# Pinned experts' weights on ScalarE's DMA queue, a ring with one more place, and the experts' weighting behind the gather

## The chip, the cores and the metric

The kernel runs on one core of a Trainium2 chip. The metric is device time in microseconds (us) of one execution, the median over several runs. The core has a matrix engine (TensorE, "PE" in the rows), three engines for elementwise work (VectorE "DVE", ScalarE "ACT", GpSimd "POOL"), and SyncE ("SP"), which issues transfers. SP and ScalarE each have a queue for plain transfers; GpSimd issues the indirect ones (gathers and scatters of rows). Every engine takes its own instructions in order.

## The reference

Two layers over a latent sequence of 512 tokens and a context of 256 tokens, width 1024, float32. Each layer has an attention and recurrence mixer and then a hierarchical mixture of experts; layer 0's mixture runs on 768 tokens, layer 1's on 512.

```python
xl = xl + ga1 * (concat([y_na, y_rg, y_diff]) @ w_out[l])
hl2 = rmsnorm(xl, g_ffn[l]) * (1 + sc2) + sh2
...
g_prob = softmax(h @ w_g + b_g)                     # 4 groups
g_top, g_idx = top_k(g_prob, 1)
e_logits = (h @ w_e + b_e).reshape(N, 4, 8)[g_idx]  # 8 experts of the group
e_top, e_idx = top_k(softmax(e_logits), 2)
weight = g_top * e_top / sum(e_top)
y[token] += weight * ((silu(x @ w1[e]) * (x @ w3[e])) @ w2[e])   # 32 experts, 1024 -> 512 -> 1024
xl = xl + ga2 * y
```

All 32 experts of a layer have tokens here, so all of w1, w3 and w2 are read: 6 MB an expert, 192 MB a layer.

## The kernel before

For each layer `program` runs a mixer, then the output projection, then the mixture of experts.

**Output projection and routing.** A loop over 128-token tiles t (six in layer 0, four in layer 1) multiplies by w_out, adds to X (`upd`, L1353), squares the row on ScalarE (L1354), takes the root on GpSimd (L1356, L1357), turns the tile for the router on TensorE with ScalarE copying the turned blocks (`turn_x`), takes the logits (L1402), and in `normed` scales (L1363) and adds the shift (L1364, on VectorE for tiles in `HVV`, else on GpSimd). SP writes the normed tile to memory (L1365). `top2` finds group and experts. After the loop come the one-hot sums: ranks of tokens within their expert, `val` and two clears of the gather buffers on GpSimd (L1439, L1441), the rank product and sum (L1442, L1448, L1449), one one-hot per half tile (L1451) times the tokens' numbers on TensorE (L1452), the experts ordered by count, and the index table `idx_t` (L1475) with `slots` (where results are scattered, L1496 to L1500), `idall` and `idn` (L1503 to L1509). `weights()` turns the router's numbers into each token's weight in its expert (L1783 to L1812): exponentials, a division, a split in three bfloat16 parts (L1795, L1797), products with the one-hots on GpSimd (L1798) and on TensorE (L1802, L1805).

**Experts.** Experts are taken in an order of slots by count. The last three slots always hold experts 29 to 31 (NPIN = 3), whatever their counts; these are called *pinned*, since their weights can be loaded before the routing is known; the order `seq` begins with them. All others are loaded by a number that routing yields (`sid`). For each slot GpSimd gathers token rows (L1832), TensorE turns them (`turn`, L1634, copied by VectorE or ScalarE through `copy`), multiplies by w1 and w3 (`first`), ScalarE and VectorE make the hidden rows (`mid` with its copy L1664, `hidden`), TensorE multiplies by w2 (`second`), and `out` scales and scatters (L1523).

**The ring of weights.** An expert's weights come in six pieces of 1 MB ([128, 2048] float32). Pieces take places in turn from three pools: `wt` (six, shared with the mixer and the projection), `wt2` (opened at the tile loop) and `wt3` (four, opened after it). `NWA` places of `NW2` are opened earlier, in the projection (`wta`); `W0` says where the six of `wt` stand in the turn. That gives 16 places in layer 0 and 18 in layer 1. `eparts` issues a piece: the first `SPIN[l]` pieces on the engine it is called with, the rest on SP. `pin_steps` yields the 18 pieces of the pinned experts: `NWA` in the projection, up to `PINT[l]` in the tile loop, then all but `HELD[l]`; the held ones wait for `idn` (L1509). A build-time planner orders each engine's instructions by when it expects them to be ready; `behind(a, b)` puts a after b on the same engine.

```python
held[0] = (Y if wcount[0] > SPIN[l] else eng).dma_start(...)          # eparts, L1030
for _ in range(8 // nt + 1):
    if wcount[0] < PINT[l]:
        next(ping)                                                   # tile loop
for _ in range(6 * NPIN - wcount[0] - HELD[l]):
    next(ping)                                                       # after the loop
```

Of the kernel before, what the change touches and what calls it, by code (L numbers as in the profile page):

```python
# [13 lines left out]
ALU = mybir.AluOpType  # L14
# [9 lines left out]
NE = 32  # L24
# [31 lines left out]
RGS = (2, 2)  # L56
RGR = (1.0, 0.85)
FLG = (1, 1)
WST = (0, 0)
HELD = (4, 3)  # L60
DMO = ("gsXw", "gsXw")
FLL = (3, 1)
LTS = ("aaatmghsscccbbbbcccccMccocHccc", "")
# [5 lines left out]
CUT = 0  # L69
W67 = ((), ())  # L70
RG0 = (5, 2)
HVV = [(1, 3), (1, 3)]
NP6 = 1
WSV = ((0, 2), (0, 2))
W1S = ((1, 1, 2, 3), (1, 1, 2, 3))
# [12 lines left out]
UE = ("SV", "SV")  # L88
OSV = ((0, 1), (0, 1))
OHV = ((0, 1, 2, 3, 4, 5), (0, 1, 2, 3, 4, 5))  # L90
SPIN = (2, 0)
PINT = (6, 8)
FEX = (0, 0)
DOR = ("asctwfv", "asctwfv")
CHD = ("TV", "TV")
# [7 lines left out]
AHEAD = 1  # L103
CXN = ((2, 0, 0), (0, 0, 2))
XNB = (6, 2)
NW2 = (6, 8)
NWA = (0, 2)
NWS = (9, 9)
W0 = (4, 12)
LAM = (1, 1)  # L110
DIAG = (1, 1)
SCT = (1, 1)
# [138 lines left out]
def program(tc, a, out, dbg=None):  # L251
    nc = tc.nc
# [22 lines left out]
    V, S, G, T = [Chained(e_) for e_ in (nc.vector, nc.scalar, nc.gpsimd, nc.tensor)]  # L275
# [69 lines left out]
        return (pool or wt).tile([128, 2048], dt, name="w", bufs=n)  # L345

    def copy(eng, o, i):
        if eng is S:
            S.copy(o, i)
        else:  # L350
            eng.tensor_copy(o, i)  # L351

    def ada_steps(l, groups=(0, 1, 2)):
        for g in groups:
# [47 lines left out]
    def behind(ins, other):  # L402
        tc.add_manual_dep(ins.ins, other.ins.name,
                          mybir.DependencyInfo(mybir.DependencyClass.NoSync, mybir.DependencyReason.DATA), reason="order")
# [6 lines left out]
    mark = {}  # L411
# [18 lines left out]
    ct = lambda c_, x_, y_: x_ if c_ else y_  # L430
# [5 lines left out]
    def bc(ap, n):  # L436
        return ap.unsqueeze(len(ap.shape)).to_broadcast(list(ap.shape) + [n])
# [13 lines left out]
    for l in range(2):  # L451
# [555 lines left out]
        lg = xp_.tile([128, nt, 36], F32, name="lg")  # L1007
# [305 lines left out]
        gm, m1, m2, t1 = [rk.tile([128, nt], F32, name=n_) for n_ in ("gm", "m1", "m2", "t1")]  # L1313
# [31 lines left out]
        op = P.open(f"op{l}", side="right")  # L1345
# [125 lines left out]
        tk = rt.tile([128, 3, 32], F32, name="tk")  # L1471
# [17 lines left out]
        nd, nm, nr = NDL[l], NML[l], NE - NPIN  # L1489
        assert (nr - nm) % 2 == 0  # L1490
        np_ = (nr - nm) // 2
        ncol = nm + np_ + NPIN
        slots = wk_.tile([128, ncol], I32, name="slots") if SCT[l] else None
        if SCT[l]:
            sf = tk[:, 2]
            V.tensor_copy(slots[:, 0:nd], sf[:, 0:nd])  # L1496
            V.tensor_copy(slots[0:64, nd:nm], sf[0:64, nd:nm])
            V.tensor_copy(slots[0:64, nm + np_:ncol], sf[0:64, nr:NE])
            for i in range(2):
                V.tensor_copy(slots[32 * i:32 * i + 32, nm:nm + np_], sf[0:32, nm + i:nr:2])  # L1500
        idall = wk_.tile([128, ncol], F32, name="idall")
        idn = wk_.tile([128, ncol, nt], F32, name="idn")
        V.tensor_copy(idall[:, 0:nd], idx_t[:, 0:nd])  # L1503
# [106 lines left out]
        class Expert:  # L1610
# [16 lines left out]
            def turn(self):  # L1627
                n = self.cap
                self.xT = wk_.tile([128, 8, 128], F32, name="xT", bufs=2)
                m = min(8, 512 // n)  # L1630
                for q in range(8 // m):
                    pt = mm()
                    for k in range(m):
                        T.transpose(pt[:, n * k:n * k + n], self.xgt[0:n, 128 * (m * q + k):128 * (m * q + k) + 128], ident[0:n, 0:n])  # L1634
                    copy(ct(q, S, V), self.xT[:, m * q:m * q + m, 0:n], pt[:, 0:n * m].rearrange("p (k t) -> p k t", t=n))
                self.p = pss()

            def first(self):
# [139 lines left out]
        wsl = rk.tile([128, nv, 32], F32, name="wsl")  # L1778
        def weights():

            gs = rt.tile([128, nt], F32, name="gs")
            gx = rt.tile([128, nt, 4], F32, name="gx")
            V.tensor_tensor(gx, lg[:, :, 0:4], bc(gm, 4), op=ALU.subtract)  # L1783
            S.activation(gx, gx, AF.Exp)
            V.tensor_reduce(gs, gx, axis=AX.X, op=ALU.add)
            V.tensor_sub(m2, m2, m1)
            S.activation(m2, m2, AF.Exp)
            V.scalar_tensor_tensor(t1, m2, 1.0, gs, op0=ALU.add, op1=ALU.mult)
            wgt = rt.tile([128, 2, nt], F32, name="wgt")
# [189 lines left out]
        for n_ in range(NE + 1):  # L1979
# [18 lines left out]
            if n_ == NE - 1:  # L1998
                mark.clear()
                if not last:  # L2000
                    for c0 in (768, 1024):
                        cut, i_ = chunk(1, c0)
# [125 lines left out]
        for k_ in SEQ[l]:  # L2128
# [4 lines left out]
            else:  # L2133
                combine(*k_)
                if k_[1]:
                    n_, t = k_[0], order[k_[0]]
# [32 lines left out]
```

## Time and profile before

| | us |
|---|---|
| median of three runs | 2021.67 |
| lowest, highest | 2017.29, 2025.94 |
| the profiled execution | 2016.25 |
| its span, first to last instruction | 2014.7 |
| TensorE busy in it | 1688.6 |
| VectorE, ScalarE, GpSimd busy | 902.0, 575.4, 405.3 |
| moved by DMA | 579.20 MB |

All times below are of the profiled execution, in us from the start of its span. Layer 0's experts run from about 520 to 1075, layer 1's from about 1486 to 1985. A busy share is an average over stages with different limits, so the stages are read by themselves. "A <- B" in a view of waits means that A sat idle until B was done; an instruction in a timeline has its start, its length, its engine and line, output <- inputs, and in brackets the idle time before it with what ended it.

### The profile page before, as it was taken

The page shows a single profiled execution, that of the slowest core. Times are in us where ns is not written, and L with a number is a line of the kernel's source. Part 1 is how long each engine was busy: PE and PEld are TensorE (multiplying, and loading weights), DVE is VectorE, ACT ScalarE, POOL GpSimd, SP SyncE. Part 2 cuts the span into 40 slices and gives each one's busy share as a digit, 9 for nine tenths or more (in the row PEclk, how much of TensorE's full clock was granted, in tenths as well). Part 3 has the DMA queues.
Part 4 walks back from the last instruction along what each step waited for, and adds up shares of the span by engine and source line. Part 5 has one row for each costly group of instructions (what it writes and reads, how often), then busy time and mean ns, then how long its engine had stood idle before and what let it go on. Part 6 is the DMA issues. An engine that isn't in the chain of part 4 may idle for free. (4 is left out here: it accounts for less than half of the span.)

```text
span 2014.7 us, 24883 instructions
## 1 busy us (share of the span) xinstructions
PE 1688.6 (84%) x9306; PEld 977.0 (48%) x9306; DVE 902.0 (45%) x1507; ACT 575.4 (29%) x1034; POOL 405.3 (20%) x395
## 2 busy tenths in 40 slices
PE   5998998898688879898985998988969988979763
PEld 3767776676333333333334866766733333323321
DVE  3877544776422222212138588648642122121225
ACT  3563454552101111111124465546311000000111
POOL 1344002443211001000003135114311110110001
PEclk8999999898798999999896999989969999999896
DMA  8537726426899989999895446454579999999994
GB/s 303 198 138 274 271 74 168 118 75 230 336 406 348 413 334 373 414 356 412 337 399 198 141 179 215 149 179 142 209 264 402 405 407 416 411 413 415 417 389 172
DMA packets 153710, 579.20 MB, mean 287 GB/s; under 512 B 18735, under 2 KB 54959, under 8 KB 114673
## 3 DMA queue, kind: packets, MB, share of 16 engines
q1 hardware_dynamic: 142240, 553.35, 72.4%
q0 software_dynamic: 9328, 20.87, 2.9%
q10 hardware_dynamic: 2016, 3.34, 0.5%
q8 instruction: 75, 1.23, 0.2%
q14 instruction: 51, 0.41, 0.1%
HBM read 544.74 MB, written 42.05 MB: 291 GB/s over the span
## 5 line engine op out<-in xcount | busy, mean ns | idle before, releaser
L497 PE MATMUL mm<-hh,w 128*128 128x256 f32 (+1 forms) x960 | 192.5, 345 | 9.2 <-ACT w L433 4.7
L1649 PE MATMUL pss<-w,xT 128*64 128x512 f32 x368 | 173.4, 619 | 7.0 <-DMA w<-in_w_dram 7.0
L1648 PE MATMUL pss<-w,xT 128*64 128x512 f32 x368 | 177.7, 626 | 0.0
L497 PEld LDWEIGHTS mm<-hh,w 128*128 128x128 f32 x960 | 151.0, 194 | 38.6 <-issue 6.4
L1644 PE MATMUL pss<-w,xT 128*32 128x512 f32 x880 | 136.8, 669 | 37.9 <-DMA w<-in_w_dram 37.7
L1832 POOL DMA_INDIRECT xg<-h2d,idx_t x64 | 61.3, 959 | 512.1 <-PE mm L1634 473.6
L1654 PE MATMUL pss<-w,xT 128*128 128x512 f32 x352 | 156.0, 598 | 0.0
L1664 ACT COPY hs<-pss 128x512 f32<-128x512 f32 x53 | 30.9, 582 | 375.7 <-PE pss L1644 224.1
L1523 POOL DMA_INDIRECT yd<-yl,slots x47 | 44.3, 942 | 382.5 <-DVE yl L1568 202.2
L1706 PE MATMUL pss<-w,hT 128*64 128x512 f32 x184 | 102.2, 699 | 9.1 <-DVE hT L1684 8.9
L1654 PEld LDWEIGHTS pss<-w,xT 128*128 128x128 f32 x352 | 65.3, 190 | 89.1 <-issue 83.5
L1684 DVE TENSOR_TENSOR hT<-hT,mm 128x128 f32<-128x128 f32 (+1 forms) x53 | 18.3, 345 | 193.8 <-ACT hT L1683 193.6
L1707 PE MATMUL pss<-w,hT 128*64 128x512 f32 x184 | 101.8, 696 | 0.0
L1564 DVE SCALAR_TENSOR_TENSOR yl<-g,wsl,yl 64x1024 f32<-64x1024 f32 (+2 forms) x32 | 40.8, 1277 | 128.7 <-ACT yl L1559 128.4
L1644 PEld LDWEIGHTS pss<-w,xT 128*32 128x32 f32 x880 | 31.5, 119 | 135.9 <-issue 72.5
L1559 ACT ACTIVATE yl<-g,wsl 64x1024 f32<-64x1024 f32 (+2 forms) x32 | 36.6, 1147 | 209.4 <-DMA yd<-yl,slots 177.3
L497 PE MATMUL mm<-hl,w 128*128 128x256 f32 (+1 forms) x480 | 92.8, 335 | 0.4 <-POOL hl L616 0.4
L1712 PE MATMUL pss<-w,hT 128*128 128x512 f32 x176 | 89.5, 655 | 3.1 <-issue 3.1
L1568 DVE TENSOR_TENSOR yl<-pss,yl 64x512 f32<-64x512 f32 (+1 forms) x44 | 29.6, 687 | 135.5 <-PE pss L1707 74.3
L351 DVE COPY xT<-mm 128x512 f32<-128x512 f32 (+1 forms) x64 | 36.2, 565 | 103.8 <-PE mm L1634 103.1
L497 PEld LDWEIGHTS mm<-hl,w 128*128 128x128 f32 x480 | 75.3, 190 | 10.4 <-POOL hl L616 0.6
L1649 PEld LDWEIGHTS pss<-w,xT 128*64 128x64 f32 x368 | 49.5, 142 | 62.6 <-issue 49.9
(380 smaller groups left out, 3256.2 us busy)
## 6 DMA issues: line engine op xcount, KB each, us to landing
w<-in_w_dram SPq DMA_DIRECT2D x382, 1024.0 KB
w<-in_w_ada_dram SPq DMA_DIRECT2D x48, 1024.0 KB
w<-in_w_in_dram SPq DMA_DIRECT2D x20, 1024.0 KB
yd<-bm SPq DMA_DIRECT2D x20, 512.0 KB
w<-yd SPq DMA_DIRECT2D x10, 1024.0 KB
ks<-st SPq DMA_DIRECT2D x16, 384.0 KB
w<-in_w_out_dram SPq DMA_DIRECT2D x5, 1024.0 KB
h2d<-hp SPq DMA_DIRECT2D x10, 512.0 KB
```

The costliest lines, as they stand in the source:

```text
L497: i_ = T.matmul(o, x_(k), y_(k), start=(n == 0), stop=(n == 23))
L1523: G.indirect_dma_start(out=yd[l][0:2 * nrow, :], out_offset=bass.IndirectOffsetOnAxis(ap=idxt, axis=0), in_=rows, in_offset=None, bounds_c ...
L1559: S.activation(self.u[r], g2[r, 1], AF.Copy, scale=b_)
L1564: (V if eng[1] == "V" else G).scalar_tensor_tensor(self.u[r], g2[r, 0], a_, self.u[r], op0=ALU.mult, op1=ALU.add)
L1644: T.matmul(ph[32 * g:32 * g + 32, 0:512], xT[:, k + g // 2, 0:32], w(k + g // 2), start=(k == 0), stop=(k == 6))
L1648: T.matmul(ph[0:64, 0:512], xT[:, k, 0:64], w1(k), start=(k == 0), stop=(k == 7))
L1649: T.matmul(ph[64:128, 0:512], xT[:, k, 0:64], w3(k), start=(k == 0), stop=(k == 7))
L1654: T.matmul(ph[:, o:o + 512], xT[:, k, :], w(k), start=(k == 0), stop=(k == 7))
L1706: T.matmul(py[0:64, :], hT[:, k, 0:64], w2(k, 0), start=(k == 0), stop=(k == 3))
L1707: T.matmul(py[64:128, :], hT[:, k, 0:64], w2(k, 1), start=(k == 0), stop=(k == 3))
L1712: T.matmul(self.p[:, 512 * hf:512 * hf + 512], hT[:, k, :], w2(k, hf), start=(k == 0), stop=(k == 3))
L1832: G.indirect_dma_start(out=o[0:n_, :], out_offset=None, in_=h2d[l][0:nrow, :], in_offset=bass.IndirectOffsetOnAxis(ap=idxt, axis=0), bound ...
```

## The change

Pins: `SPIN` 18 sends all 18 pinned pieces of a layer through ScalarE's queue, `PINT` 14 asks for up to 14 of them by the end of the tile loop, and `HELD` leaves one (layer 0) or none (layer 1) for after `idn`. Ring: one more early place in each layer (`NW2`, `NWA`), 17 and 19 places, with the `wt` places at other turns (`W0`); the memory comes from a smaller scratch for the descriptors of GpSimd's transfers. Routing: the casts of `slots` and the steps of `weights()` on VectorE go behind the first copy of the first expert's turned rows (`mark["V", "xT"]`), and the eight steps of that expert's `first` stand ahead of `weights()` in the program (`WST` 8). The shift add L1364 goes to VectorE for tiles 4 and 5 in layer 0 and tile 2 in layer 1 (`HVV`).

```diff
-WST = (0, 0)
-HELD = (4, 3)
+WST = (8, 8)
+HELD = (1, 0)
-HVV = [(1, 3), (1, 3)]
+HVV = [(1, 3, 4, 5), (1, 2, 3)]
-SPIN = (2, 0)
-PINT = (6, 8)
+SPIN = (18, 18)
+PINT = (14, 14)
-NW2 = (6, 8)
-NWA = (0, 2)
+NW2 = (7, 9)
+NWA = (1, 3)
-W0 = (4, 12)
+W0 = (7, 9)
...
     def copy(eng, o, i):
-        if eng is S:
-            S.copy(o, i)
-        else:
-            eng.tensor_copy(o, i)
+        return S.copy(o, i) if eng is S else eng.tensor_copy(o, i)
...
         slots = wk_.tile([128, ncol], I32, name="slots") if SCT[l] else None
-        if SCT[l]:
-            sf = tk[:, 2]
-            V.tensor_copy(slots[:, 0:nd], sf[:, 0:nd])
-            V.tensor_copy(slots[0:64, nd:nm], sf[0:64, nd:nm])
-            V.tensor_copy(slots[0:64, nm + np_:ncol], sf[0:64, nr:NE])
-            for i in range(2):
-                V.tensor_copy(slots[32 * i:32 * i + 32, nm:nm + np_], sf[0:32, nm + i:nr:2])
...
-                    copy(ct(q, S, V), self.xT[:, m * q:m * q + m, 0:n], pt[:, 0:n * m].rearrange("p (k t) -> p k t", t=n))
+                    i_ = copy(ct(q, S, V), self.xT[:, m * q:m * q + m, 0:n], pt[:, 0:n * m].rearrange("p (k t) -> p k t", t=n))
+                    if q == 0:
+                        mark["V", "xT"] = i_
...
         def weights():
 
+            m_ = mark["V", "xT"]
+            if SCT[l]:
+                sf = tk[:, 2]
+                behind(V.tensor_copy(slots[:, 0:nd], sf[:, 0:nd]), m_)
+                V.tensor_copy(slots[0:64, nd:nm], sf[0:64, nd:nm])
+                V.tensor_copy(slots[0:64, nm + np_:ncol], sf[0:64, nr:NE])
+                for i in range(2):
+                    V.tensor_copy(slots[32 * i:32 * i + 32, nm:nm + np_], sf[0:32, nm + i:nr:2])
             gs = rt.tile([128, nt], F32, name="gs")
             gx = rt.tile([128, nt, 4], F32, name="gx")
-            V.tensor_tensor(gx, lg[:, :, 0:4], bc(gm, 4), op=ALU.subtract)
+            behind(V.tensor_tensor(gx, lg[:, :, 0:4], bc(gm, 4), op=ALU.subtract), m_)
             S.activation(gx, gx, AF.Exp)
             V.tensor_reduce(gs, gx, axis=AX.X, op=ALU.add)
-            V.tensor_sub(m2, m2, m1)
+            behind(V.tensor_sub(m2, m2, m1), m_)
...
-    nc = bacc.Bacc("TRN2", target_bir_lowering=False, num_devices=1)
+    nc = bacc.Bacc("TRN2", target_bir_lowering=False, num_devices=1, dynamic_dma_scratch_size=4096)
```

## Rows read from the trace of the kernel before

**Rows 1.** TensorE's waits, 520 to 1075: us in total, times, longest.

```profile
PE mm L1678 <- ACT hs L1664: 43.5, 12, 7.3
```

**Rows 2.** TensorE's waits, 1486 to 1985.

```profile
PE pss L1644 <- DMA w<-in_w_dram: 37.7, 16, 4.4
```

**Rows 3.** Waits of SP's queue, 1486 to 1985.

```profile
SPq L1030 <- DMA w<-in_w_dram: 308.1, 151, 6.8
```

**Rows 4.** Windows: engines' busy us (instructions), granted clock, DMA share, GB/s.

```profile
1485.00:1490.00 5.00, 1.89 (x16) 1.80 (x16) 2.11 (x11) 0.00 (x0) 2.60 (x3) 0.50 0.51 152
...
1500.00:1505.00 5.00, 5.00 (x26) 1.76 (x24) 0.62 (x2) 2.25 (x3) 0.87 (x1) 1.00 0.70 231
...
1600.00:1700.00 100.00, 83.98 (x461) 35.64 (x463) 23.49 (x39) 8.78 (x18) 10.47 (x11) 0.94 1.02 411
```

**Rows 5.** VectorE in order of time, layer 0, 440 to 545.

```profile
474.44 1.94 DVE L1364 TENSOR_TENSOR hp<-hp,w 128x1024 f32<-128x1024 f32 x1
...
492.36 2.93 DVE L1326 TENSOR_TENSOR e<-em,m 128x128 f32<-128x128 f32 x1
...
497.99 0.29 DVE L1326 TENSOR_TENSOR e<-em,m 128x128 f32<-128x128 f32 x1
...
502.64 0.25 DVE L1402 SCALAR_TENSOR_TENSOR lg<-acc,r,crow 128x36 f32<-128x36 f32 x1 [1.23 <-PE acc L1380]
502.81 1.63 DVE L1329 TENSOR_TENSOR oh<-e,t 128x128 bf16<-128x128 f32 x1
...
508.81 0.22 DVE L1341 TENSOR_TENSOR ohb<-oh 128x128 bf16<-128x128 bf16 x1
...
510.20 1.33 DVE L1795 CAST w3p<-wgt 128x12 bf16<-128x12 f32 x1
...
513.32 0.31 DVE L1442 TENSOR_SCALAR yl<-oh,pidx 128x384 bf16<-128x384 bf16 x1
513.55 0.54 DVE L1448 TENSOR_TENSOR yl<-oh,mm 128x384 f32<-128x384 bf16 x1
...
514.41 0.53 DVE L1449 TENSOR_REDUCE pos<-yl 128x12 f32<-128x384 f32 x1
...
515.03 2.04 DVE L1451 TENSOR_SCALAR oneh<-iob,pos 128x128 bf16<-128x128 bf16 x12
...
518.95 0.19 DVE L1475 TENSOR_TENSOR idx_t<-tk 128x32 int32<-128x32 f32 x1
```

**Rows 6.** GpSimd in order of time, layer 0: clears of gather buffers, first gather.

```profile
509.66 1.84 POOL L1441 MEMSET xg<- 128x1024 f32 x2
...
520.04 1.24 POOL L1832 DMA_INDIRECT xg<-h2d,idx_t  x1 [5.73 <-DVE slots L1500]
```

**Rows 7.** VectorE in order of time, layer 1, 1425 to 1520.

```profile
1458.06 2.75 DVE L1327 TENSOR_TENSOR e<-e,cs 128x64 f32<-128x64 f32 x1
...
1474.15 0.22 DVE L1341 TENSOR_TENSOR ohb<-oh 128x128 bf16<-128x128 bf16 x1
...
1479.94 0.40 DVE L1448 TENSOR_TENSOR yl<-oh,mm 128x256 f32<-128x256 bf16 x1
```

**Rows 8.** TensorE in order of time, layer 0: the weights' product.

```profile
524.39 1.51 PE L1802 MATMUL mm<-oneh,yl 128*96 128x128 bf16 x12
```

**Rows 9.** DMA issues from 519 to 521: count, us from issue to landing.

```profile
xg<-h2d,idx_t POOLq DMA_INDIRECT x1, 3.2
```

**Rows 10.** DMA issues of the whole span: count, median us to landing.

```profile
xg<-h2d,idx_t POOLq DMA_INDIRECT x64, 6.4
```

**Rows 11.** SP's queue in order of time, layer 0.

```profile
504.73 2.54 SPq L1030 DMA_DIRECT2D w<-in_w_dram  x4
```

**Rows 12.** SP's queue in order of time, layer 1.

```profile
1470.42 2.36 SPq L1030 DMA_DIRECT2D w<-in_w_dram  x4
...
1486.52 11.20 SPq L1030 DMA_DIRECT2D w<-in_w_dram  x4
```

**Rows 13.** ScalarE in order of time, layer 0: last tile's turned copies.

```profile
498.33 0.59 ACT L349 COPY xT<-mm 128x512 f32<-128x512 f32 x1
```

## Prediction

> **What bounds the kernel now.** I read the waits of TensorE first, then those of SP's queue, then the busy time by windows around the start of each mixture-of-experts stage, and last the instructions of that start in order of time. In layer 0's stage (520 to 1075 us) TensorE's longest group of waits is for the ScalarE copy of the hidden rows, 43.5 us in 12 waits [rows 1]; no row of that answer has it wait for an expert's weights. Layer 0 is bound by the engines. In layer 1's stage (1486 to 1985 us) the same view is headed by the weights, 37.7 us in 16 waits [rows 2], and SP, which issues them, spent 308.1 us waiting for earlier loads to land [rows 3]. From 1600 to 1700 the DMA share is 1.02 at 411 GB/s [rows 4]. Layer 1 is bound by the stream of weights. So the two layers price this change differently: in layer 0 only what brings TensorE's first expert forward counts; in layer 1 what counts is how early the stream can run without a gap, and how many pieces are in store by then.
>
> At layer 1's start the stream has gaps: share 0.51 from 1485 to 1490 and 0.70 from 1500 to 1505 [rows 4], because the ring is full and places come free only when TensorE works. TensorE has half its clock there (granted 0.50 at 1485 to 1490, 1.00 at 1500 to 1505). So the routing chain that leads to the first expert is on the path in both layers: logits, top two, one-hot sums, the index, the gather, transposes, first matmul.
>
> **Part by part.** *Steps for the experts' weights moved behind the turn of the first expert's rows (and the eight first-half steps of that expert ahead of them).* Layer 0: the one-hot of the last tiles ends at 509.03; VectorE then works on the experts' weights until L1442 at 513.32, the rank product L1448 starts only at 513.55, and the twelve one-hots L1451 at 515.03 [rows 5]. With those steps gone the chain is held by GpSimd's two clears of the gather buffers, 509.66 to 511.50 [rows 6]: a cast begun at 510.20, in the middle of them, took 1.33 us and ended with them [rows 5]. If the one-hots start at 511.50 the gain is 3.5 us; if L1442 too is held until 511.50, then it, L1448 and the sum L1449 (0.31, 0.54 and 0.53 us) come first, and the gain is 2.1. I take 3.0, plus 0.3 for three small steps that stood further up: 3.3. Layer 1: from 1474.37 to 1479.94 VectorE has 5.6 us [rows 7], of which ten steps of the routing itself take 2.0; 3.6 is freed (2.4 to 3.9 by the same two cases).
>
> The five casts of slots also go behind, but they stand after the index (its end is 519.14, the gather's start 520.04 [rows 5, 6]). If the gather was let go by the index, they cost it nothing; if by the last cast, 0.7 us. I take 0.
>
> On TensorE the weights' product no longer stands between turn and first matmul: L1802 took 1.51 us [rows 8], 0.6 of it after the turned rows were ready, and its follower 0.4: 1.0 in layer 0, 0.8 in layer 1 (0 to 1.9 each). The same steps now must end before the first expert's result is scaled. In layer 0 they share ScalarE with the hidden-row copy, and one more stall of the kind in rows 1 costs 43.5/12 = 3.6 us. I take 1.5 off (0 to 3.6). In layer 1 nothing is scaled ahead, so 0.
>
> *Shift add of tiles 4 and 5 (layer 0) and 2 (layer 1) from GpSimd to VectorE.* On VectorE it takes 1.94 us; but beside GpSimd's add a VectorE step of normally 0.29 us took 2.93, and another 1.63 [rows 5]. Tile 4: 2.6 lost now against 1.9 spent, +0.7. Tile 5: 1.3 lost now; of the 1.9 spent, 1.2 fills the wait for the logits ahead of 502.64; +0.6. Layer 0: 1.3 (0 to 2.0). Layer 1: 2.75 [rows 7] where layer 0's like step takes 0.29, against 1.9: +0.6, and 0.1 for the write that goes out sooner: 0.7 (-1.9, if the step is placed where nothing waits now, to 1.4). Behind the added work VectorE queues the next tile's update and the top two; if the add is placed late, the write of the tile to memory is late, but the gather is over 10 us off.
>
> The Trainium skill speaks against this step ("SBUF — State Buffer", Who interferes with whom): two-input VectorE work and GpSimd's reads share a port pair, and whoever issues first blocks the other for the whole instruction. By that rule the three adds could hold GpSimd's next root step by up to 1.9 us each, and the sum would be 5.8 us worse at most; the rows above show the blocking, in the direction that now costs VectorE.
>
> *One more place.* A piece of 1,048,576 bytes takes 2.55 us at 411 GB/s [rows 4]. In layer 1 the store is one piece larger when the ring is full: 2.55 us, provided the place is filled before TensorE frees the first. Layer 0 does not wait for weights: 0 (up to 2.5 in its tail). The smaller scratch for GpSimd's descriptors that pays for the place shows nowhere in this trace; nearest is the time from a gather's issue to landing, 3.2 us unloaded and 6.4 in the median of 64 [rows 9, 10]. I take 0, and 6.4 - 3.2 = 3.2 per layer as its bad end.
>
> *Pins through ScalarE's queue, none or one held.* SP is in order: four pins went out at 504.73 right behind the last tile's write, and in layer 1 four at 1470.42 and three more, held for the index, from 1486.52 [rows 11, 12]. On ScalarE's queue they need not stand behind those writes. By itself I price the queue at 0: the pins are needed later than they land in either order. What it does is fill all places before the gather. Two things can go wrong. First, what is queued behind a pin that waits on ScalarE is the squares and the turned copies of the next tile (a rival below). Second, the gather met drained queues so far, because pins were held until the index: 3.2 us, against 6.4 in the median [rows 9, 10]. With places filled earlier the queues should be nearly drained again by about 514 and 1480; I take 0.5 off per layer (0 to 3.2).
>
> **Sum.** Layer 0: 3.3 + 1.3 + 1.0 - 1.5 - 0.5 = 3.6 us. Layer 1: 3.6 + 0.7 + 0.8 + 2.55 - 0.5 = 7.15 us. Together 10.75 us off the profiled execution's 2016.25: 2005.5. The median of the runs shown is 2021.67, 5.4 us above that execution, so for a median I predict 2021.67 - 10.75 = 2010.9, rounded to 2011. Late next in layer 0 is the ScalarE copy of rows 1, in layer 1 the stream.
>
> **Rivals.** (a) *ScalarE held by pins: slower.* A pin whose place is freed by a tile's norm may stand ahead of that same tile's turned copies. Tile 5's copies start at 498.33 [rows 13], and the pin behind its norm went out at 504.73 [rows 11]: up to 6.4 us held. A like hold at tile 3 of each layer, taken at the same price, makes three, 19 us; add a wait for an earlier load to land, at worst 6.8 us [rows 3], in each layer: 32.8 us together, against 10.75 gained, 22 slower: 2043. It decides for a slower kernel from 10.75 us of holds, for a measurable one from 21. For: ScalarE is in order and does this work now. Against: the order is made at build time by when things are expected to be ready, and a place freed by the norm is ready after the copies. 0.10.
> (b) *The gather meets the pins.* Latency 6.4 instead of 3.2 in both layers: 2 x 2.7 us more than I took off. Gain 5.3: 2016. For: three fewer pins are held. Against: the queues are idle for long stretches before. 0.13.
> (c) *The queue changes nothing and the place is not filled in time*, because pins go out as late as now: 2.55 lost: gain 8.2, 2013.5. 0.10. By the Trainium skill ("DMA: Bandwidth & Descriptors", Issuing engines are not separate DMA queues) a second issuing queue saves no more than the issue time, which points to this case; the rows at 504.73 and 1470.42 show order, not issue time, as what SP costs the pins.
> (d) *More than the sum:* the place also pays in layer 0, because scatters land sooner in a queue that is less pressed. The 43.5 us of rows 1 are waits of that kind; a quarter less gives 11 more: 2000. Against: the bytes are the same. 0.12.
>
> **How the numbers follow.** The forecast has 0.55. Some 0.5% (10 us) is what a measurement of this kernel can tell from no change, so the border for faster is 2011.6, next to the forecast: its own range, 2003 to 2018 (bounds of the unknown costs, partly cancelling), lies 0.37 below and 0.18 above. With (d), faster 0.37 + 0.12 = 0.49; same 0.18 + 0.13 + 0.10 + 0.01 from (a) = 0.42; slower 0.09. The range for 8 in 10 reaches up over (b) and (c) with their spread, 2022, and down to most of (d), 1999; the rest is (a) and part of (d).
>
> **What would show it.** Right: the last steps of the experts' weights after the first turned copy on VectorE, the one-hots L1451 starting some 4.5 us sooner counted from the last tile's logits, the gather landing in 3 to 4 us, layer 1's share at 1.0 from about 7 us sooner counted from the stage's start, no ScalarE idle time that ends with a pin. Wrong: idle time of ScalarE ahead of the squares or copies of a tile; a first gather of 6 us; a layer 0 stage longer than before by stalls at the hidden-row copy.

## The result, and the profile of the changed kernel

The changed kernel took 2037.02 us in the median of ten runs (2028.24 to 2042.43), the kernel before 2022.93 in ten (2009.78 to 2028.30): a ratio of 1.0076, 95% interval 1.0055 to 1.0097. It is 0.8% slower, where 2011 was forecast and 1999 to 2022 was the range. The profiled execution took 2041.68 us with a span of 2040.1, that of before 2016.25.

The table cuts both profiled executions, and those of all experiments below, at the same instructions. "Mixer" runs from TensorE's first product with yh to its first product of ks and qs, the start of the differential attention. "Logits" runs from the first product of the projection to the last tile's logits, "gather" from there to the first gather, "turn" to the first turned row, "first" to the first matmul of an expert, "experts" to the last product with w2. "End" is the rest of the span. The ratio is to the kernel before, each from runs on the same chip.

| | mixer 0 | logits 0 | gather 0 | turn 0 | first 0 | experts 0 | mixer 1 | logits 1 | gather 1 | turn 1 | experts 1 | end | ratio (95%) |
|---|---|---|---|---|---|---|---|---|---|---|---|---|---|
| before | 13.0 | 60.8 | 17.1 | 3.3 | 2.5 | 534.2 | 11.7 | 40.0 | 17.1 | 3.0 | 491.1 | 33.4 | 1 |
| after | 20.5 | 72.1 | 12.6 | 3.2 | 1.9 | 543.6 | 27.9 | 43.9 | 11.3 | 5.0 | 485.6 | 29.1 | 1.0076 (1.0055-1.0097) |
| scratch alone | 20.6 | 60.7 | 16.8 | 3.4 | 2.5 | 546.8 | 19.2 | 40.0 | 16.7 | 3.2 | 489.7 | 29.0 | 1.0029 (1.0002-1.0055) |
| after + unused tile | 13.4 | 70.4 | 12.6 | 3.1 | 1.9 | 536.7 | 21.0 | 43.8 | 11.3 | 4.8 | 486.9 | 29.2 | 0.9993 (0.9974-1.0011) |
| the same, shift adds back | 13.3 | 72.1 | 12.6 | 3.2 | 2.0 | 533.9 | 19.4 | 45.9 | 11.3 | 4.7 | 486.0 | 29.2 | 1.0012 (0.9988-1.0037) |
| routing alone | 13.1 | 55.9 | 13.6 | 8.5 | 1.9 | 544.8 | 11.9 | 40.0 | 15.2 | 3.2 | 489.1 | 32.7 | 0.9994 (0.9968-1.0021) |
| tile + early pins on SP | 12.6 | 71.3 | 12.6 | 3.1 | 1.9 | 542.4 | 11.4 | 43.8 | 11.3 | 4.9 | 485.3 | 29.1 | 0.9949 (0.9927-0.9970) |
| the same, 12 pins in the loop | 12.7 | 67.2 | 12.6 | 6.1 | 1.9 | 536.1 | 11.5 | 43.8 | 11.3 | 4.9 | 486.5 | 29.0 | 0.9946 (0.9926-0.9966) |
| the same, without the place | 12.7 | 72.4 | 12.6 | 3.1 | 1.9 | 548.9 | 10.7 | 44.1 | 11.3 | 3.0 | 488.7 | 29.1 | 1.0008 (0.9983-1.0033) |
| tile + all pins on SP | 12.6 | 61.9 | 17.0 | 7.1 | 1.9 | 537.8 | 11.7 | 38.6 | 15.4 | 5.9 | 487.0 | 29.1 | 0.9950 (0.9922-0.9979) |
| - without the place | 13.1 | 61.2 | 17.0 | 6.0 | 1.9 | 542.0 | 10.7 | 38.6 | 15.5 | 6.9 | 490.0 | 29.1 | 0.9993 (0.9970-1.0016) |
| - shift adds back | 12.6 | 58.0 | 16.2 | 7.2 | 1.9 | 535.5 | 11.6 | 40.0 | 15.2 | 6.4 | 485.3 | 29.0 | 0.9958 (0.9934-0.9982) |
| - routing back | 12.7 | 61.2 | 19.9 | 5.3 | 2.5 | 531.8 | 11.3 | 38.7 | 17.3 | 5.9 | 485.3 | 28.8 | 0.9951 (0.9930-0.9972) |
| all on SP, pins held | 13.1 | 61.2 | 17.0 | 3.9 | 1.9 | 536.6 | 11.5 | 38.7 | 15.4 | 3.2 | 486.6 | 29.2 | 0.9919 (0.9893-0.9946) |
| - shift adds back | 12.8 | 63.5 | 16.3 | 3.3 | 1.9 | 537.8 | 11.6 | 40.0 | 15.2 | 3.0 | 488.3 | 29.0 | 0.9928 (0.9903-0.9954) |
| - routing back | 12.7 | 61.9 | 19.7 | 3.3 | 2.5 | 531.6 | 11.0 | 38.6 | 16.9 | 2.9 | 488.1 | 29.1 | 0.9910 (0.9886-0.9933) |
| - without the place | 12.8 | 61.9 | 17.0 | 3.4 | 1.9 | 544.5 | 11.0 | 38.7 | 15.5 | 3.1 | 489.1 | 29.1 | 0.9924 (0.9899-0.9949) |

From before to after the two mixers lose 7.5 + 16.2 = 23.7 us, a stretch that the prediction never looked at. Layer 0's logits come 11.3 us later; the way from logits to gather is 4.5 and 5.8 us shorter, as the routing part was meant to do; layer 1's experts take 5.5 us less and the end 4.3. Layer 0's experts take 9.4 us more, and here the two executions differ beyond the change. The windows of this stage, before and then after (stretch, length, busy us of TensorE, its weight loads, VectorE, ScalarE, GpSimd, then the granted clock, DMA share, GB/s):

```profile
525.84:1060.07 534.23, 464.22 (x2035) 183.93 (x2034) 129.69 (x186) 75.58 (x111) 52.51 (x55) 0.93 0.96 378
```

```profile
538.14:1081.74 543.60, 479.79 (x2046) 187.38 (x2046) 133.02 (x199) 75.80 (x113) 56.02 (x60) 0.91 0.95 372
```

TensorE idles less after (543.6 - 479.8 = 63.8 us against 70.0) and is busy 15.6 us longer at a lower clock. Over the table's executions this stage takes 531.6 to 542.0 us where its granted clock was 0.93 or 0.94, and 542.4 to 548.9 where it was 0.91 or 0.92; which of the two makes the other is not shown. The 9.4 us of this stage would account for most of the 11.3 by which the two profiled executions (25.4 us apart) differ more than the medians (14.1).

**The mixers.** Waits of TensorE, first before (1320 to 1370 us), then after (1340 to 1410): us in total, times, longest.

```profile
PE pss L267 <- DMA X<-xd: 2.4, 1, 2.4
```

```profile
PE pss L267 <- DMA ks<-st: 18.7, 1, 18.7
```

After the change TensorE stood for 18.7 us until ks had landed. The queues in order of time show why (ga, qs, ks and X are loads for the differential attention and the projection behind it; rh is a tile of the local attention and recurrence). First SP and VectorE of before, layer 1:

```profile
1320.98 0.33 SPq L1075 DMA_DIRECT2D ga<-ada  x1
1325.61 1.75 SPq L1054 DMA_DIRECT2D qs<-st  x4
...
1339.86 1.51 DVE L968 TENSOR_TENSOR yT<-yT,rh 128x512 f32<-128x512 f32 x1 [1.27 <-ACT rh L967]
...
1341.39 1.73 SPq L1054 DMA_DIRECT2D ks<-st  x4
```

and then VectorE, SP and ScalarE's queue after:

```profile
1359.39 1.51 DVE L965 TENSOR_TENSOR yT<-yT,rh 128x512 f32<-128x512 f32 x1 [1.26 <-ACT rh L964]
...
1360.92 0.33 SPq L1072 DMA_DIRECT2D ga<-ada  x1
1361.36 2.29 SPq L1051 DMA_DIRECT2D qs<-st  x4
1367.22 4.57 SPq L1051 DMA_DIRECT2D ks<-st  x4
1378.73 6.02 SPq L1068 DMA_DIRECT2D X<-xd  x4
...
1360.94 0.35 ACTq L1027 DMA_DIRECT2D w<-in_w_dram  x1
1366.77 0.34 ACTq L1027 DMA_DIRECT2D w<-in_w_dram  x1
1369.10 0.34 ACTq L1027 DMA_DIRECT2D w<-in_w_dram  x1
```

In the kernel before, ga went out at 1320.98 and qs at 1325.61, and only ks waited for VectorE's last step on rh (1339.86 + 1.51 = 1341.37, ks at 1341.39). After, already ga goes out at the end of that step (1359.39 + 1.51 = 1360.90, ga at 1360.92), and qs, ks and X stand behind it in SP's order. Three pins go out on ScalarE's queue among them, and SP waits 11.3 us for pins to land before it has issued X:

```profile
SPq L1068 <- DMA w<-in_w_dram: 11.3, 2, 6.9
```

Layer 0 shows the first half alone: qs moved from 304.30 to 325.52, right behind VectorE's last step on rh.

**The last tile of layer 0.** ScalarE, TensorE, VectorE and GpSimd after, in order of time:

```profile
504.54 11.23 ACTq L1027 DMA_DIRECT2D w<-in_w_dram  x2
515.87 0.59 ACT L348 COPY xT<-mm 128x512 f32<-128x512 f32 x1 [15.07 <-DVE hp L1361]
...
506.55 1.90 PE L1377 MATMUL acc<-wra,xT 128*128 128x36 f32 x8 [7.45 <-DVE lg L1399]
...
510.28 1.52 PE L1370 MATMUL mm<-cst,X 128*128 128x128 f32 x6
516.50 3.63 PE L1377 MATMUL acc<-wra,xT 128*128 128x36 f32 x16 [4.71 <-ACT xT L348]
...
513.49 1.89 DVE L1361 TENSOR_TENSOR hp<-hp,w 128x1024 f32<-128x1024 f32 x1
...
520.18 0.26 DVE L1399 SCALAR_TENSOR_TENSOR lg<-acc,r,crow 128x36 f32<-128x36 f32 x1 [4.80 <-PE acc L1377]
...
526.99 2.04 DVE L1448 TENSOR_SCALAR oneh<-iob,pos 128x128 bf16<-128x128 bf16 x12
...
533.04 1.24 POOL L1832 DMA_INDIRECT xg<-h2d,idx_t  x1 [7.37 <-DVE sid L1479]
```

The second of two pins issued from 504.54 waited until VectorE's last shift add ended (513.49 + 1.89 = 515.38). The two turned copies stood behind it: ScalarE idled 15.07 us before the first, which it made at 515.87 although TensorE had turned the tile by 511.80; some 4 us of the 15.07 are the hold, and the logits waited 4.71 us for it. Before that TensorE had already waited 7.45 us for VectorE to take an earlier tile's logits out of their bank.

### The profile page after: what moved, and what is told of

Its sections match the earlier page's. It is cut to its first block, busy times and chain, and to the rows that moved or that the text cites. A ratio compares the mean times of both kernels' runs of the same rounds, so it can differ in the third digit from the quotient of the medians.

```text
span 2040.1 us, 24894 instructions
## 1 busy us (share of the span) xinstructions
PE 1703.2 (83%) x9306; PEld 974.1 (48%) x9306; DVE 900.0 (44%) x1510; ACT 573.4 (28%) x1034; POOL 409.4 (20%) x392
## 3 DMA queue, kind: packets, MB, share of 16 engines
q1 hardware_dynamic: 135808, 517.70, 67.2%
## 4 chain that ended last, share of the span: by engine, by line
PE 32%; DMA 27%; issue 21%; DVE 10%; ACT 4%; POOL 4%; SPq 0%; POOLq 0%; ACTq 0%; DVEq 0%
DMA w<-in_w_dram 19%; PE mm L494 10%; DMA yd<-yl,slots 3%; PE acc L267 3%; PE pss L267 2%; PE pss L1646 1%; DMA w<-in_w_ada_dram 1%; PE mm L267 1%; PE pss L1636 1%; PE pss L1640 1%; DVE tt L778 1%; PE mm L586 1%; PE acc L359 1%; PE po L919 1%; PE mm L877 1%
## 5 line engine op out<-in xcount | busy, mean ns | idle before, releaser
L1832 POOL DMA_INDIRECT xg<-h2d,idx_t x64 | 61.4, 960 | 487.0 <-PE mm L1624 453.3
L1698 PE MATMUL pss<-w,hT 128*64 128x512 f32 x184 | 105.6, 721 | 10.4 <-DVE hT L1676 10.1
L1699 PE MATMUL pss<-w,hT 128*64 128x512 f32 x184 | 104.4, 712 | 0.0
L1676 DVE TENSOR_TENSOR hT<-hT,mm 128x128 f32<-128x128 f32 (+1 forms) x53 | 18.2, 344 | 182.4 <-ACT hT L1675 182.1
L1636 PEld LDWEIGHTS pss<-w,xT 128*32 128x32 f32 x880 | 31.2, 121 | 135.4 <-issue 72.4
L267 DVE TENSOR_REDUCE mn<-pss 128x1 f32<-128x768 f32 (+1 forms) x80 | 64.0, 840 | 35.9 <-PE pss L267 35.6
```

What stands on the lines that cost most here:

```text
L267: i_ = f(*a_, **k_)
L1636: T.matmul(ph[32 * g:32 * g + 32, 0:512], xT[:, k + g // 2, 0:32], w(k + g // 2), start=(k == 0), stop=(k == 6))
L1698: T.matmul(py[0:64, :], hT[:, k, 0:64], w2(k, 0), start=(k == 0), stop=(k == 3))
L1699: T.matmul(py[64:128, :], hT[:, k, 0:64], w2(k, 1), start=(k == 0), stop=(k == 3))
L1832: G.indirect_dma_start(out=o[0:n_, :], out_offset=None, in_=h2d[l][0:nrow, :], in_offset=bass.IndirectOffsetOnAxis(ap=idxt, axis=0), bound ...
```

## The experiments

The unused tile in what follows is 12,288 bytes a partition, by which the smaller scratch had moved the tiles on the low side of the memory. Differences in us are differences of ratios times 2022.

### The scratch alone

```
-    nc = bacc.Bacc("TRN2", target_bir_lowering=False, num_devices=1)
+    nc = bacc.Bacc("TRN2", target_bir_lowering=False, num_devices=1, dynamic_dma_scratch_size=4096)
```

> The kernel before with one edit: the smaller scratch for the descriptors of GpSimd's transfers (4096 instead of 16384 bytes a partition). No pin, place, or step is moved. Theory M (memory): all tiles on the low side of SBUF move down by 12,288 bytes while those on the high side stay, so the loads for the differential attention (ga, qs, ks) come to lie over tiles of the local attention that are read later, and SP, which is in order, issues them later: about 20 us later in both layers, TensorE's first product of ks and qs 5 to 8 us later in layer 0 and 8 to 17 us later in layer 1; in all 13 to 25 us slower, 2036 to 2048. Theory Q (queue): what delayed these loads in the changed kernel were the pins on ScalarE's queue, which are not here: 2023, no change, and ga, qs and ks issued at the same times as before.

Ratio 1.0029 (1.0002 to 1.0055), 0.4 to 11 us slower. Both mixers lose, 7.6 us (theory M: 5 to 8) and 7.5 (8 to 17). SP's queue in layer 1, its wait and TensorE's:

```profile
1361.69 0.33 SPq L1075 DMA_DIRECT2D ga<-ada  x1
1362.13 1.79 SPq L1054 DMA_DIRECT2D qs<-st  x4
1363.96 2.79 SPq L1054 DMA_DIRECT2D ks<-st  x4
```

```profile
SPq L1075 <- DVE yT L968: 27.6, 1, 27.6
```

```profile
PE pss L267 <- DMA X<-xd: 10.0, 1, 10.0
```

Here ga is held until VectorE's last step on rh ends, and goes out 1.1 us behind TensorE's first product with yh (1360.58), where before the change it went out 19.3 us ahead of it (1340.28), and there is no pin near it. The time rose by less than the 13 us that were expected at least: 7.6 + 7.5 less the 4.3 us that the same edit takes off the end (last section) is 10.8. Theory Q, no change, falls by the issue times; the time itself only just leaves it out.

### The addresses of before given back to the changed kernel

```
         nap = P.open(f"na{l}")
+        padp = P.open(f"pad{l}")
+        padp.tile([128, 3072], F32, name="pad")
...
         att.release()
+        padp.release()
```

> The changed kernel with an unused tile of 12,288 bytes a partition below the tiles of the local attention and recurrence of each layer, so that these have the addresses that they had before the change; queue, pins, places and routing as changed. Theory M: ga, qs and ks are issued as early as before the change; the mixers give back 6 us in layer 0 and 10 to 17 us in layer 1, the rest of it being transfers that share the 16 engines with the three pins that now go out there: 2037 less 16 to 23, that is 2014 to 2021. Theory Q: nothing of the mixers' loss comes back, 2037.

Ratio 0.9993 (0.9974 to 1.0011): of the changed kernel's 1.0076, 16.8 us come back, at the lower end of what theory M had. Layer 0's mixer is whole again (13.4). In layer 1 ga goes out early, yet 21.0 us remain instead of 11.7:

```profile
1324.98 1.42 SPq L1075 DMA_DIRECT2D ga<-ada  x1
1328.55 4.13 SPq L1054 DMA_DIRECT2D qs<-st  x4
1344.33 8.26 SPq L1054 DMA_DIRECT2D ks<-st  x4
...
1344.35 0.37 ACTq L1030 DMA_DIRECT2D w<-in_w_dram  x1
1350.23 0.35 ACTq L1030 DMA_DIRECT2D w<-in_w_dram  x1
1352.55 0.33 ACTq L1030 DMA_DIRECT2D w<-in_w_dram  x1
```

The four issues of ks stretch over 8.26 us, 1.73 before, with three pins going out on ScalarE's queue in the same time. Most of that is no issuing but a wait of SP until a pin had landed (waits of SP's queue, 1340 to 1356):

```profile
SPq L1054 <- DMA w<-in_w_dram: 6.0, 1, 6.0
```

So memory and queue share the loss of layer 1's mixer: 7.5 us for the one alone, 9.3 for the other alone, 16.2 for both.

### The early pins on SP's queue

```
-                    held[0] = (Y if wcount[0] > SPIN[l] else eng).dma_start(...)
+                    held[0] = (Y if wcount[0] > SPIN[l] or wcount[0] <= NWA[l] else eng).dma_start(...)
```

> The changed kernel with the unused tile of 12,288 bytes, and the pins of the early places (one in layer 0, three in layer 1) back on SP's queue, where they stand behind the loads of the mixer. Theory C (sharing): with the unused tile alone, TensorE in layer 1 still had 21.0 us from its first product with yh to its first product of ks and qs (11.7 before the change), because three pins on ScalarE's queue went out among the loads of ks and shared the engines with them. On SP they follow these loads: the distance falls to 11.7 to 13 us, the time by 8 us against the unused tile alone, 2012. Rival: the three pins are then missing at the start of layer 1's experts and the stream gives the 8 us back there: 2019 to 2021 with the distance at 12 us.

Ratio 0.9949 (0.9927 to 0.9970), 8.9 us under the run with the unused tile alone. Layer 1's mixer takes 11.4 us, ks is issued in 1.92:

```profile
1346.61 1.92 SPq L1054 DMA_DIRECT2D ks<-st  x4
...
1395.92 2.08 SPq L1030 DMA_DIRECT2D w<-in_w_dram  x3
```

The pins now go out at 1395.92, and layer 1's experts lose nothing by that (485.3). That the three pins made this loss stands; theory C's mechanism, sharing the engines, is not all of it. In the run before this one 6.0 us were SP's wait for a pin, which is gone here; from the last issue of ks to TensorE's product it took 11.6 us there (1352.59 to 1364.21) and 8.3 here (1348.53 to 1356.87). Why a load on one queue waits for a pin on the other to land, no run shows.

### The held copies: 12 pins in layer 0's loop

```
-PINT = (14, 14)
+PINT = (12, 14)
```

> As the run with early pins on SP, and at most 12 pins asked for by the end of layer 0's tile loop instead of 14, so that the pin whose place the last tile's norm frees stands behind that tile's two turned copies on ScalarE. Theory H (holding): that pin held ScalarE, and with it the last logits: 9 to 10 us from the first product of the projection to the last logits come back in layer 0 (70.4 us with the unused tile alone, 60 to 61 here), 2002 to 2004. Rival B: the gather, now 10 us earlier, meets the pins still under way and takes 6 to 9 us to land instead of 3: 4 to 5 us of it stay, 2007 to 2009.

Ratio 0.9946 (0.9926 to 0.9966): no gain over the run above. The logits come 4.1 us sooner, 67.2 instead of 71.3, and the gather then takes 6.1 us to its turn instead of 3.1. ScalarE no longer holds a copy that TensorE has ready:

```profile
500.62 0.58 ACT L348 COPY xT<-mm 128x512 f32<-128x512 f32 x1 [10.22 <-PE mm L1373]
501.42 0.58 ACT L348 COPY xT<-mm 128x512 f32<-128x512 f32 x1 [0.21 <-PE mm L1373]
505.06 2.92 ACTq L1030 DMA_DIRECT2D w<-in_w_dram  x5
```

So the hold was there, but priced at 9 to 10 us by theory H it was worth 4; the rest of the late logits is TensorE's 7.45 us for the logits' bank, which this run has too. Rival B is right on what becomes of the gain.

### All pins on SP's queue

```
-SPIN = (18, 18)
+SPIN = (0, 0)
```

> The changed kernel with the unused tile of 12,288 bytes and all 18 pins of each layer on SP's queue; nothing is issued on ScalarE's. Theory S (the queue itself is worth nothing): pins stand behind the mixer's loads and hold no copy, so both losses of ScalarE's queue are gone and the time is that of the run with early pins on SP and at most 12 pins in the loop, within 3 us: 2002 to 2009. Rival: SP in its turn is held by pins whose places are not free, and the writes of the normed tiles stand behind them: the gather of layer 0 starts no sooner than with the unused tile alone, 2012 to 2020.

This is the changed kernel with the unused tile, without ScalarE's queue: 0.9950 (0.9922 to 0.9979), the same as the two above, as theory S has it. The logits are back at 61.9 and 38.6 us, and both mixers at 12.6 and 11.7. With the logits goes more than the hold: in all traces with most pins on ScalarE's queue TensorE waits for VectorE at the logits of both layers (7.4 and 6.7 us with the unused tile alone), and in none with all pins on SP. What in VectorE's steps makes these waits is not separated. Two things replace that gain: from logits to gather it takes 17.0 us instead of 12.6, since work that was done while the logits were late now stands on the path, and the turn waits for the gather:

```profile
515.28 1.24 POOL L1835 DMA_INDIRECT xg<-h2d,idx_t  x1 [7.68 <-DVE sid L1482]
...
522.43 1.08 PE L1627 MATMUL mm<-cst,xg 64*128 64x64 f32 x8 [7.93 <-DMA xg<-h2d,idx_t]
...
501.61 2.72 SPq L1030 DMA_DIRECT2D w<-in_w_dram  x4
```

### Pins held for the gather

```
-HELD = (1, 0)
+HELD = (4, 3)
```

> As the run with all pins on SP (2009.5 us), with as many pins held for after the index as before the change: four in layer 0, three in layer 1. Theory B (the gather meets the pins): in that run the first gather took 7.2 us until TensorE's turn in layer 0 and 5.9 in layer 1, against 3.3 and 3.0 before the change; with the pins held it takes 3 to 3.5 again in both, and 4 to 6 us of 6.7 come back: 2004 to 2006. Rival: the held pins leave gaps in layer 1's stream (three pieces at 2.55 us), which cost there what the gather gains: 2009 to 2013, with layer 1's experts 3 us or more longer.

On top of the run above: 0.9919 (0.9893 to 0.9946), 2004.85 us, 16.4 us faster than the kernel before (11 to 22). This version beats both kernels. The 6.3 us to the run above lie within the two intervals, and it is the stages that carry theory B: the turn comes 3.9 and 3.2 us after the gather instead of 7.1 and 5.9, and the held pins leave no loss in layer 1's experts (486.6):

```profile
517.30 1.24 POOL L1835 DMA_INDIRECT xg<-h2d,idx_t  x1 [7.68 <-DVE sid L1482]
...
521.21 1.08 PE L1627 MATMUL mm<-cst,xg 64*128 64x64 f32 x8 [4.70 <-DMA xg<-h2d,idx_t]
...
503.63 0.91 SPq L1030 DMA_DIRECT2D w<-in_w_dram  x1
```

### The routing part

Alone, on the kernel before (the diff's hunks for `slots`, `weights()`, `mark` and `WST`, nothing else):

> The kernel before with the routing part of the change alone: casts of slots and the steps of the experts' weights behind the first turned copy, the eight first-half steps of the first expert ahead of them. Theory R (the gain in the chain is real and stays): the one-hots start 4 to 5.5 us sooner after the last tile's logits in both layers, and 8 to 10 us stay in the end: 2013 to 2015. Rival: layer 0 gives its part back later, because there TensorE waits for scatters and the hidden-row copy and not for its start: only layer 1's 4 to 5.5 us stay, 2017 to 2019.

Ratio 0.9994 (0.9968 to 1.0021), no difference shown; the rival is nearer than theory R. The logits come 4.9 us sooner in layer 0 and the gather 3.5 us sooner behind them, but the turn takes 8.5 us instead of 3.3: this gather starts at 508.65, the last four pins went out at 496.90. Undone in the run with all pins on SP, and in the one with pins held:

> As the run with all pins on SP (2009.5 us), with the casts of slots and the steps of the experts' weights back at their old place ahead of the gather. Theory R: the chain from the projection to the gather gets 4 to 8 us longer in each layer; in layer 1 all of this stays, in layer 0 the gather then meets fewer pins and 3 us of it come back: 2015 to 2020. Rival: the start of the experts is not what counts, since the ring is full and the stream of weights restarts when TensorE frees places: at most 3 us slower, 2010 to 2012.5.

> As the run with all pins on SP and pins held for the gather (2004.9 us), with the casts of slots and the steps of the experts' weights back ahead of the gather. Theory R2 (the move is worth what it takes off the chain, and without held pins a gather that met the pins gave part of it back): 3.5 us longer to the first matmul in layer 0 and 2.0 in layer 1, 5 us slower, 2009 to 2011. Rival: it is worth nothing in the time, because TensorE's first expert is not what the stage waits for: 2004 to 2006.

Ratios 0.9951 (0.9930 to 0.9972) against 0.9950, and 0.9910 (0.9886 to 0.9933) against 0.9919. On the chain the move is worth most of its price in layer 0 and half of it in layer 1: 2.9 and 1.9 us from the logits to the gather, and 0.6 more to the first matmul in layer 0 (2.7, 1.4 and 0.6 with pins held). In the time nothing of it is seen, either way. In both pairs layer 0's experts take 5 to 6 us longer with the move (537.8 and 536.6 against 531.8 and 531.6), and with the routing alone 10.6 longer than before (544.8 against 534.2), which is more than its gain there. The granted clock of the stage is lower with the move in two of the three (0.93 against 0.94, 0.92 against 0.93), and single executions spread by more than 6 us, so this is not shown to be the reason.

### The shift adds

Back on GpSimd, on three bases:

```
-HVV = [(1, 3, 4, 5), (1, 2, 3)]
+HVV = [(1, 3), (1, 3)]
```

> As the run with the unused tile of 12,288 bytes, and the shift adds of tiles 4 and 5 (layer 0) and 2 (layer 1) back on GpSimd. Theory V: on VectorE the added 1.9 us each delay the copy of the logits out of their bank, for which TensorE then waited 7.5 us in layer 0 and 6.7 us in layer 1: 3 to 8 us faster than the run with the unused tile alone. Rival P: the loss in layer 0's routing is the pin that stands in ScalarE's queue ahead of the last tile's turned copies and waits for that tile's last shift add; on GpSimd this add ends no sooner, so layer 0 stays as it was or gets up to 3 us worse, and only layer 1's 2 to 4 us come back: 1 to 4 us faster.

> As the run with all pins on SP (2009.5 us), with the shift adds of tiles 4 and 5 (layer 0) and 2 (layer 1) back on GpSimd. Theory: on VectorE they are worth 2 to 4 us, as between the two runs with the unused tile (2020.5 with, 2024.3 without): 2011.5 to 2013.5. Rival: that difference came from the order on ScalarE's queue; with the pins on SP there is none: within 1 us.

> As the run with all pins on SP and pins held for the gather (2004.9 us), with the shift adds of tiles 4 and 5 (layer 0) and 2 (layer 1) back on GpSimd. With nothing held, putting them back shortened the chain from the projection to the gather by 4.7 us in layer 0 and lengthened it by 1.3 in layer 1, and the time did not change. Theory A (the adds on VectorE cost layer 0 more than they gain in layer 1, and the gather that met the pins hid it): 3 us faster, 2001 to 2002. Rival (the prediction's own price): 2 us slower, 2007.

Ratios 1.0012 against 0.9993, 0.9958 against 0.9950, 0.9928 against 0.9919: slower by 3.8, 1.6 and 1.8 us, each within the intervals. In layer 1 the chain to the gather is 2.1, 1.3 and 1.1 us longer without the added shift adds; in layer 0 it moves by +1.6, -4.7 and +1.5. Theory V, by which VectorE's adds made TensorE wait 7.5 us for the logits' bank, falls: without them that wait is only 1.8 us shorter (5.6 against 7.4), and TensorE waits 8.8 us for ScalarE's turned copies instead of 5.3.

### The additional place

Taken away on three bases, with the pins in the loop and those held fitted to the smaller ring:

```
-NW2 = (7, 9)
-NWA = (1, 3)
-W0 = (7, 9)
+NW2 = (6, 8)
+NWA = (0, 2)
+W0 = (6, 8)
```

> As the run with at most 12 pins by the end of layer 0's tile loop, without the additional place: 16 and 18 places, two of them early in layer 1 and none in layer 0, two pins of layer 0 held for after the index. Theory G (the place pays its price in layer 1 alone): 2.6 to 5 us slower than that run, all of it in layer 1's experts. Rival: the place also covers stalls in layer 0: 8 us or more slower. Rival: it pays nothing, since it is not filled in time: within 1 us.

> As the run with all pins on SP (2009.5 us), without the additional place (16 and 18 places, two pins of layer 0 held). Without the place the time on ScalarE's queue rose by 14.8 us, more than any theory gave. Theory G2 (place): it shortens TensorE's idle time in layer 0's experts by 4 us, and the length of layer 1's by 3.5 us, so 7 to 8 us slower, 2017. Rival: 12 us or more slower, if layer 0 depends on the place more than its idle time shows. Rival: 2 to 4 us slower, if the 14.8 us came from the order on ScalarE's queue and not from the place.

> As the run with all pins on SP and pins held for the gather (2004.9 us), without the additional place. Theory G3: the place is worth 3 us in layer 1's experts and 4 to 9 us in layer 0's, as in the two pairs before (14.8 and 12.1 us in the medians): 2012 to 2018. Rival: with pins held the places are not full at the index anyway, so the additional one is filled late and pays 3 us or less: 2005 to 2008.

Ratios 1.0008 against 0.9946, 0.9993 against 0.9950, 0.9924 against 0.9919: 12.5, 8.7 and 1.0 us. In the first pair the held copies are back too, and the logits of layer 0 come 5.2 us later. Layer 1's experts take 2.2, 3.0 and 2.5 us longer without it, each time about the price of one piece. What the place does in layer 0 is not settled: experts there take 12.8, 4.2 and 7.9 us longer without it in the profiled executions (TensorE busy 6.9, 2.9 and 5.6 us longer and idle 6.0, 1.3 and 2.3), at a granted clock of 0.92, 0.93 and 0.92 against 0.93, and where pins are held the difference in the time is 1.0 us with intervals that leave some 7 either way.

## Why the prediction was wrong

The step that failed is the one on the scratch: "shows nowhere in this trace", priced at 0 with 3.2 us a layer as its bad end, by the latency of a gather. A smaller scratch also moves what lies above it. The tiles of the local attention and recurrence slid under the loads of the differential attention, these loads waited for later readers, and SP, in order, passed the wait on: 7.6 and 7.5 us of the mixers with this edit alone. Undoing that in the changed kernel gives back 16.8 us, as much as the 15.4 that were lost. The trace of before shows where to look: ks went out 0.02 us after VectorE's last step on rh, a load that waits for memory, with ga and qs free of it.

The second is "By itself I price the queue at 0: the pins are needed later than they land in either order." That asked when pins are needed, not what they meet. On SP they stood behind the mixer's loads; on ScalarE three went out among them and cost 8.9 us in layer 1. The page of the Trainium skill that the prediction named for rival (c) ("DMA: Bandwidth & Descriptors", Issuing engines are not separate DMA queues) says also that transfers of different issuers interleave on the same engines. That ks took 11.6 us from its last issue to the product beside three pins, and 8.3 without them, fits this; the 6.0 us that SP itself waited for a pin to land it doesn't tell. The prediction used only the half on issue time, which fits too (0.9946 with the later pins on ScalarE's queue, 0.9950 with all on SP's). The prediction went from stage to stage of the experts and never read the mixers, though `NWA` puts places and pins there.

Rival (a) had the right mechanism with the wrong weight: the pin behind the last norm held the turned copies of layer 0, not for 6.4 us at three tiles but for 4 at one. Its sign was the one that the prediction named, idle time of ScalarE ahead of a tile's copies, 15.07 us. Its 2043 lies near the 2037 by another road. Rival (b) is right where the chain gets shorter: 7.1 and 5.9 us to the turn with one pin or none held, 8.5 with the routing alone. In the changed kernel layer 0 escaped it (3.2) because its gather was late, and layer 1 paid 2.0 against the 0.5 taken off. Rival (c) falls with the 2.2 to 3.0 us that the place is worth in layer 1. Rival (d) put the 43.5 us of rows 1 down to scatters, but that row names ScalarE's copy of the hidden rows; what the place does in layer 0 stays open.

Term by term, of the sum of 10.75 us: the routing part on the chain 3.3 + 1.0 in layer 0 and 3.6 + 0.8 in layer 1, measured 2.9 + 0.6 and 1.9 + 0.2 [rows 5, 7 and 8 for what they replace]. The 4.5 and 5.8 us by which the way from logits to gather shrank in the changed kernel overstate it, since those logits were late. The one-hots start 6.6 us behind the last logits instead of 12.1, the sign that was named. The stall of 1.5 us doesn't show: TensorE's waits for the hidden-row copy of layer 0 are 35.6 us in 11 after and 37.3 in 11 with the routing alone, against 43.5 in 12. The shift adds, 1.3 and 0.7: the sign in layer 0 is open, layer 1 gives 1 to 2. The place, 2.55 in layer 1: 2.2 to 3.0, as the stream's rate said [rows 4]. Layer 1's experts gained 5.5 us in the changed kernel, all of it out of sight behind 23.7 us of mixers.

With both faults mended and pins held the edit is worth 16.4 us. That it is more than 10.75 is no proof of the sum. The chain on which most of the sum stood gained nothing in layer 0, where logits, gather, turn and first add up to 84.0 us against 83.7 before, and 2.8 us in layer 1 (57.3 against 60.1 to the turn). Taking away the routing part, the shift adds or the place leaves 14.6 to 18.2 us. The profiled executions are 10.8 us apart: 4.2 us are the shorter end and 3.5 lie between mixer and projection in layer 0, where X is loaded from 300 us on instead of 327, neither of them forecast; 4.5 are layer 1's experts and 2.8 the chain there, and layer 0's experts take 2.4 back. Part of the time goes with the granted clock: it was 0.914 in the mean of this version's six runs and 0.909 in the 29 of the kernel before beside them, and among those 29 a run at 0.01 less takes some 12 us longer, by which I estimate 7 of the 16.4 us. Whether the edit raised the clock is not shown.

## What to carry to other kernels

A change of memory is a change of order: what is freed or shrunk moves every tile above it, and a load whose tile now lies over a later reader holds all that is queued behind it. Look in the trace for loads that go out the moment some other step ends, and keep the addresses of such neighbours when something is resized. A transfer that moves to an idle queue loses the order that the busy queue gave it: ask which loads it now goes out among, whether any of them waits for it to land, and which computing step stands behind it on the new engine.

## What the runs showed of the hardware that was not expected

GpSimd's closing drain depends on the size of the scratch. The instructions of the program's last line, before, after and with the scratch alone (duration in ns, least/median/longest):

```profile
L2165 POOLq DRAIN  x3: 46/112/10132, 2003.7 to 2014.4; - x3
```

```profile
L2165 POOLq DRAIN  x3: 46/113/3767, 2033.3 to 2039.8; - x3
```

```profile
L2165 POOLq DRAIN  x3: 46/113/3764, 2029.7 to 2036.0; - x3
```

10.13 us with the scratch of before (10.06 in the run with the routing alone), 3.77 and 3.76 with 4096 bytes; with the longer one the program ends 4.3 us later behind its last product.

VectorE can hold GpSimd as GpSimd holds VectorE [rows 5]. In the changed kernel, GpSimd's root steps, the first alone, the next beside VectorE's norm of a tile, the last beside two shift adds:

```profile
497.27 0.19 POOL L1353 TENSOR_SCALAR r<-ss 128x1 f32<-128x1 f32 x1
...
498.13 2.04 DVE L1360 SCALAR_TENSOR_TENSOR hp<-X,r,w 128x1024 f32<-128x1024 f32 x1 [2.88 <-POOL r L1354]
498.18 1.93 POOL L1353 TENSOR_SCALAR r<-ss 128x1 f32<-128x1 f32 x1
...
502.56 3.69 DVE L1361 TENSOR_TENSOR hp<-hp,w 128x1024 f32<-128x1024 f32 x2
502.74 2.05 POOL L1354 TENSOR_TENSOR r<-r,mhalf 128x1 f32<-128x1 f32 x1
```

A step of 0.19 us on one column took 1.93 and ended with VectorE's. That is what the Trainium skill says of the shared port pair ("SBUF — State Buffer", Who interferes with whom), in the direction that the prediction held against the shift adds. Here it is the norm that holds GpSimd, which the kernel had before. But the other root step, 0.54 us alone, took 2.05 beside the two shift adds, one of which the change put there: 1.5 us, where the prediction allowed 1.9.

The time from a first gather to the turn of its rows is 2.9 to 3.9 us where as many pins are held as before, and 5.3 to 7.2 us where fewer are and no late logits gave the others time to land. The routing alone holds as many as before and still has 8.5 us in layer 0: its gather starts 11.8 us behind the issue of four pins, 15.3 before.
